# Three plain chunks in the first FFN, and high parts sent out alone in all FFN layers

## The chip, the cores and the metric

The kernel runs on one core of one Trainium2 chip. The metric is the time of one execution on the device in microseconds. Three runs of the kernel before took 1061.67, 1060.71 and 1061.58 us, median 1061.58.

## What is computed

Two decoder layers over 256 tokens of width 1024, in float32: a half-step FFN, an attention mixer (FoX in layer 0, latent attention MLA in layer 1, with a key/value side computed once between), a second half-step FFN and a gated per-layer input, each followed by a layer norm.

```python
def swiglu(x, w_in, w_out):
    h = x @ w_in
    gate, up = h[..., :D_FF], h[..., D_FF:]
    return (jax.nn.silu(gate) * up) @ w_out

for i in range(DEPTH):                       # DEPTH = 2
    if i == N_A:                             # N_A = 1
        k_nope, k_rope, v_shared = shared_kv(x, kv_w_down, kv_norm, kv_w_up, cos, sin)
    x = post_norm(x, 0.5 * swiglu(x, ffn1_w_in[i], ffn1_w_out[i]), ln_g[i, 0], ln_b[i, 0])
    if i < N_A:
        mix = fox_mixer(x, fox_w_in[i], fox_b_f[i], fox_w_o[i])
    else:
        mix = mla_mixer(x, ..., k_nope, k_rope, v_shared, cos, sin)
    x = post_norm(x, mix, ln_g[i, 1], ln_b[i, 1])
    x = post_norm(x, 0.5 * swiglu(x, ffn2_w_in[i], ffn2_w_out[i]), ln_g[i, 2], ln_b[i, 2])
    gate = jax.nn.sigmoid(x @ ple_w_gate[i] + ple_b_gate[i])
    x = post_norm(x, gate * (p[i] @ ple_w_proj[i]), ln_g[i, 3], ln_b[i, 3])
```

post_norm is LN(sqrt(2) * x + delta). D_FF is 2816.

## The kernel before

**Products in three parts.** Each float32 operand of a product is split into a high part (a copy rounded to the matmul's format, made by ScalarE) and a low part (the rest, a subtraction on VectorE). A product is then three matmuls: high by high, high by low, low by high (mm3, L581). So every weight costs ScalarE a "high" and VectorE a "low" before TensorE can use it.

**The stream of weights.** Class Stream (L145) loads weight groups of 1 MB by SyncE's DMA queue, three groups ahead, into raw tiles, and splits them unit by unit (128 x 1024) into ten slots hl0 to hl9 (and homes such as ota, otb, qk, fs when they are lent). A slot comes free once its last product is issued. When the split of a unit is written into the program is decided while the program is generated: after every product, pump (L357) looks at a small clock model. pe_t, act_t and dve_t are the planner's times of TensorE, ScalarE and VectorE; busy (L339) adds to them, for VectorE a fixed 150 ns and 1.05 ns an element. If the raw weight has arrived and the later of act_t and dve_t is at most 1600 ns (SLACK_NS) ahead of pe_t, pump issues the next split (split, L218), both parts together. split(half=True) issues the high alone and leaves the low as self.rest, which later (L208) issues; before the change that is called only by ahead (L192), from close (L801) and from a few places of the mixers' hand-written orders FOX (L49) and ORDER (L71), where "a" is ahead, "l" is later and "f n" fills n units. use (L369) splits at once whatever is still missing when a product needs it. Each engine works through its instructions strictly in the order written.

**An FFN** (ffn, L697) has 11 chunks of 256 hidden columns. HT (L781) computes the gate and the up product of a chunk (each 48 matmuls of 256 columns), close (L801) multiplies silu(gate) by up on VectorE. What follows depends on the chunk:
- plain: the chunk's hidden values are split, and W (L904) multiplies them by w_out at the end of the FFN: 24 matmuls of 512 columns for both token tiles.
- summed: seven products in place of eight (21 matmuls) on sums. add (L814) forms differences of the hidden values (L818, L822, L823) and splits a form of 896 columns; Stream.add (L267) adds up w_out's blocks on VectorE (L273, L279, L281) and then splits four units "ws" (three of 1024 elements, one of 512, in the order 1, 0, 2, 3). sums (L833) then runs the products of a batch of chunks into seven PSUM banks, and product 4 is added to x right away (L858).

In the first FFN (cold) chunk 0 comes first, then the gate and up products of chunks 1 to 4, batch 1 of the sums, chunks 5 to 7, batch 2, chunks 8 to 10 (always plain, STAG = 3), then W. The other FFNs start with both token tiles of chunks 0 and 1 (H, L708) and go on in the same way. Which of the first eight chunks are plain is the tuple early (L705).

Of the kernel before, what the change touches and what calls it, by code (L numbers as in the profile page):

```python
# [28 lines left out]
SLACK_NS = 1600.0  # L29
# [115 lines left out]
class Stream:  # L145


    def __init__(self, nc, raw_pool, pool, loads, seq):
        self.nc, self.raw_pool, self.pool, self.loads = nc, raw_pool, pool, loads
        seen = []  # L150
        self.groups = []
        for key in seq:
            g = group_of(key)
            if g not in seen:
                seen.append(g)
                self.groups.append(g)
        members = {g: [] for g in self.groups}
        self.left = {}
        for key in seq:
            if key not in self.left:  # L160
                self.left[key] = 0
                members[group_of(key)].append(key)
            self.left[key] += 1
        self.order = [k for g in self.groups for k in members[g]]
        self.index = {k: i for i, k in enumerate(self.order)}
        self.last_of = {members[g][-1]: i for i, g in enumerate(self.groups)}
        self.raw, self.hl, self.sums, self.added = {}, {}, {}, {}
        self.slots = [f"hl{i}" for i in range(NSLOT)]
        self.slot_of = {}
        self.kept = set()  # L170
        self.loaded = self.ready = 0
        self.done = 0
        self.pending = None
        self.pe_t = self.act_t = self.dve_t = self.dma_t = 0.0
        self.arrives = {}
        self.between = {}
        self.hold = False
        self.rest = None
        self.at = 0
        self.stop = None  # L180

    def load(self, n=NRAW):
        while self.loaded < len(self.groups) and self.loaded < self.done + n:
# [34 lines left out]
    def split(self, half=False):  # L218
        self.later()
        nc = self.nc  # L220
        key = self.order[self.ready]
        g = group_of(key)
        while self.sums_left(key):
            self.add(g)
        src, parts, n = unit_of(key, self.raw[g], self.sums.get(g))
        slot = self.slots.pop(0)
        self.slot_of[key] = slot
        w = self.place(key, slot)
        hi, lo = w[:parts, 0, :n], w[:parts, 1, :n]
        shape = src.shape  # L230
        if len(shape) == 3:
            hi = hi.rearrange("p (a b) -> p a b", b=shape[2])
            lo = lo.rearrange("p (a b) -> p a b", b=shape[2])
        elif len(shape) == 4:
            hi = hi.rearrange("p (a b c) -> p a b c", b=shape[2], c=shape[3])
            lo = lo.rearrange("p (a b c) -> p a b c", b=shape[2], c=shape[3])
        t = self.arrives[group_of(key)]
        self.act_t, self.dve_t = max(self.act_t, t), max(self.dve_t, t)

        def both():  # L240
            nc.scalar.activation(hi, src, AF.Copy)  # L241
            nc.vector.tensor_tensor(lo, src, hi.bitcast(F32), op=ALU.subtract)  # L242

        if key[0] == "pb":
            nc.gpsimd.memset(w[:, 0, :].bitcast(F32), 0.0)
            lo = w[32:33, 0, :n]
            both()
        elif half:
            nc.scalar.activation(hi, src, AF.Copy)  # L249
            self.busy(act=n)  # L250

            def rest():
                nc.vector.tensor_tensor(lo, src, hi.bitcast(F32), op=ALU.subtract)  # L253
                self.busy(dve=n)
                self.split_done(key, w)

            self.rest = rest
            return
        else:
            both()  # L260
        self.pair(n)
        self.split_done(key, w)
# [76 lines left out]
    def busy(self, act=0, dve=0, pe=0):  # L339
# [1 line left out]
        if act:  # L341
            self.act_t = max(self.act_t, self.pe_t) + 200 + 0.84 * act
        if dve:
            self.dve_t = max(self.dve_t, self.pe_t) + 150 + 1.05 * dve
        if pe:
            self.pe_t += max(109, 0.437 * pe + 4)

# [8 lines left out]

    def pump(self):  # L357

        if self.ready == len(self.order) or not self.slots or self.hold or self.order[self.ready] == self.stop:
            return  # L360
        arrival = self.arrives.get(group_of(self.order[self.ready]), 1e12)
        if arrival <= self.pe_t + 500 and max(self.act_t, self.dve_t) <= self.pe_t + SLACK_NS:
            key = self.order[self.ready]
            if self.sums_left(key):
                self.add(group_of(key))
            else:
                self.split()

    def use(self, key):  # L369
        self.retire()  # L370
        self.load()
        i = self.index[key]
        self.at = max(self.at, i + 1)
        while self.ready <= i:
            assert self.slots, (key, self.slot_of)
            self.split()
            self.pe_t = max(self.pe_t, self.dve_t)
# [106 lines left out]
class Trunk:  # L484
# [212 lines left out]
    def ffn(self, li, which, lni, kv=False, ple=False, at=None, cold=False, after=()):  # L697
# [4 lines left out]
        g, gT, forms = {}, {}, {}  # L702
        homes = HOMES[:3] if kv else HOMES
        S.reclaim(*homes)
        early = (0,) if cold else (0, 1) if kv else (1,)  # L705
        summed = [c for c in range(NCH - STAG) if c not in early]

        def H(c, t, at=None, what=None, sweeps=0):  # L708
# [272 lines left out]
        for c in range(n - STAG, n):  # L981
            W(c, (1,), next_x if c == n - 1 else None)
        self.ln(1, z[1], 1.0, 4 * LN_EPS)

    def room(self, c, summed):
        self.full[c] = f = self.tl([128, 1024], F32, "P", 2)
# [913 lines left out]
```

## Time and profile before

| | us |
|---|---|
| median of three runs | 1061.58 |
| the profiled execution itself | 1060.52 |
| its span in the trace | 1058.7 |

The span runs from the first to the last instruction on the core; the 1.8 us between it and the execution's time lie around it. Times in the trace count from the span's start. The stages as the trace shows them, by the start of their first products:

| stage | from us |
|---|---|
| first FFN, batch 1 of the sums | 60.7 |
| its chunks 5 to 7 | 84.7 |
| batch 2 | 117.8 |
| chunks 8 to 10, then W | 137.5 |
| FoX mixer | 193.3 |
| second FFN of layer 0 | 309.6 |
| second FFN of layer 1 | 841.9 |

PE is TensorE, DVE VectorE, ACT ScalarE. A row of the timeline gives start, length, engine, line, operation, output<-inputs, how many in a row, and in brackets how long the engine was idle before and what released it. Matmuls overlap, so a row's length is more than the time from one start to the next. A window row gives its stretch, its length, an engine's busy time and the TensorE clock granted (1.00 is full).

### The profile page before, as it was taken

The numbers are of one execution on the slowest core, as the hardware profiler recorded it, in microseconds if no ns is written. First come the engines' busy times: TensorE is split into PE (matmuls) and PEld (weight loads), VectorE is DVE, ScalarE is ACT, GpSimd is POOL, SyncE is SP. The second block draws the span as 40 slices with busy tenths as digits, with TensorE's granted clock in tenths as the row PEclk, the third lists the DMA queues.
The fourth block names the chain that finished last, engine by engine and source line by source line (L and its number), as shares of the span: only waits on it lengthen the run. The fifth ranks groups of instructions, "written<-read, shape, count | busy, mean of one in ns | idle before, by whom it ended". The sixth has DMA issues, their size and how long they took to land.

```text
span 1058.7 us, 17610 instructions
## 1 busy us (share of the span) xinstructions
PE 1037.5 (98%) x7091; PEld 949.4 (90%) x7091; DVE 883.9 (83%) x1296; ACT 587.0 (55%) x893; POOL 58.3 (6%) x88
## 2 busy tenths in 40 slices
PE   9999899999999999999999999999999999999996
PEld 8979799898878989998889999988999889899986
DVE  5897887868888889977978799778888889899776
ACT  6555465457846464663564646526776474655631
POOL 0000000113400000000040000000000000000000
PEclk9999999999999999999999999999999999999998
DMA  7846367446447465664575646642444465556522
GB/s 280 316 160 217 141 236 252 155 142 225 161 148 264 174 210 199 212 229 168 207 256 182 210 149 229 232 134 105 136 169 151 168 238 200 187 196 224 205 115 80
DMA packets 37477, 202.74 MB, mean 191 GB/s; under 512 B 3970, under 2 KB 9874, under 8 KB 16532
## 3 DMA queue, kind: packets, MB, share of 16 engines
q1 hardware_dynamic: 37396, 201.63, 53.6%
q8 instruction: 55, 0.90, 0.3%
q14 instruction: 26, 0.21, 0.1%
HBM read 200.55 MB, written 1.06 MB: 190 GB/s over the span
## 4 chain that ended last, share of the span: by engine, by line
PE 70%; ACT 2%; DVE 1%; issue 1%; DVEq 0%; ACTq 0%
PE h L589 37%; PE y L589 23%; PE tr L589 8%; PE tr L593 2%; PE h L593 0%; ACT P L1310 0%; ACT hl L241 0%; ACT qk L602 0%; ACT xT L1603 0%; DVE hl L242 0%; DVE x L681 0%; DVE tr L1685 0%; ACT L570 0%; ACT L757 0%; DVE y L1292 0%
## 5 line engine op out<-in xcount | busy, mean ns | idle before, releaser
L589 PE MATMUL h<-xT,hl 128*128 128x256 f32 x3408 | 394.8, 277 | 0.3 <-DVE hl L302 0.3
L589 PEld LDWEIGHTS h<-xT,hl 128*128 128x128 f32 x3408 | 391.8, 188 | 1.4 <-ACT xT L602 0.6
L242 DVE TENSOR_TENSOR hl<-raw,hl 128x1024 fp32r<-128x1024 f32 (+3 forms) x290 | 338.1, 1197 | 49.0 <-ACT hl L241 47.6
L241 ACT ACTIVATE hl<-raw 128x1024 fp32r<-128x1024 f32 (+3 forms) x290 | 287.7, 1031 | 77.3 <-DVE raw L281 21.9
L589 PE MATMUL y<-hl,g 128*128 128x512 f32 x396 | 92.5, 391 | 0.0
L589 PEld LDWEIGHTS y<-hl,g 128*128 128x128 f32 x396 | 73.7, 188 | 14.8
L589 PE MATMUL y<-hl,otb 128*128 128x512 f32 x264 | 69.3, 395 | 0.0
L589 PE MATMUL h<-hl,xT 128*128 128x512 f32 (+2 forms) x306 | 67.1, 371 | 1.4 <-ACT hl L241 1.4
L589 PEld LDWEIGHTS h<-hl,xT 128*128 128x128 f32 x306 | 53.4, 188 | 11.7 <-ACT hl L241 2.5
L589 PEld LDWEIGHTS y<-hl,otb 128*128 128x128 f32 x264 | 48.1, 188 | 9.5 <-DVE otb L606 0.3
L253 DVE TENSOR_TENSOR hl<-raw,hl 128x1024 fp32r<-128x1024 f32 (+2 forms) x42 | 50.0, 1195 | 2.2 <-ACT hl L249 2.1
L589 PE MATMUL y<-hl,ota 128*128 128x512 f32 x192 | 49.9, 393 | 0.0
L673 POOL TENSOR_TENSOR rs<-ve,mhalf 128x1 f32<-128x1 f32 x16 | 15.1, 943 | 623.5 <-DVE ve L672 623.5
L602 ACT ACTIVATE xT<-tr 128x512 fp32r<-128x512 f32 x28 | 16.1, 596 | 58.2 <-PE tr L593 58.2
L242 DVE TENSOR_TENSOR hl<-ts,hl 128x1024 fp32r<-128x1024 f32 (+1 forms) x52 | 48.0, 962 | 0.2 <-ACT hl L241 0.2
L249 ACT ACTIVATE hl<-raw 128x1024 fp32r<-128x1024 f32 (+2 forms) x42 | 43.1, 1029 | 7.1 <-DVE raw L281 6.1
L589 PE MATMUL tr<-xT,hl 128*128 128x256 f32 x384 | 45.3, 277 | 0.0
L589 PEld LDWEIGHTS tr<-xT,hl 128*128 128x128 f32 x384 | 44.5, 188 | 0.4
L589 PE MATMUL y<-hl,xT 128*128 128x512 f32 (+3 forms) x228 | 43.9, 340 | 0.0
L797 ACT ACTIVATE P<-h 128x512 f32<-128x512 f32 x33 | 19.6, 594 | 41.4 <-PE h L589 41.1
L241 ACT ACTIVATE hl<-ts 128x1024 fp32r<-128x1024 f32 (+1 forms) x52 | 41.9, 839 | 0.0
L589 PEld LDWEIGHTS y<-hl,ota 128*128 128x128 f32 x192 | 34.9, 188 | 6.6
(284 smaller groups left out, 1459.3 us busy)
## 6 DMA issues: line engine op xcount, KB each, us to landing
raw<-in_ffn_in_dram SPq DMA_DIRECT2D x85, 1024.0 KB, 4.9
raw<-in_ffn_out_dram SPq DMA_DIRECT2D x44, 1024.0 KB, 5.0
raw<-in_pg_dram SPq DMA_DIRECT2D x8, 1024.0 KB, 5.6
raw<-in_mo_dram SPq DMA_DIRECT2D x8, 1024.0 KB, 4.7
raw<-in_kq_dram SPq DMA_DIRECT2D x8, 640.0 KB, 4.5
gb<-in_ln_g_dram SPq DMA_DIRECT2D x8, 512.0 KB, 6.7
gb<-in_ln_b_dram SPq DMA_DIRECT2D x8, 512.0 KB, 6.3
raw<-in_fk_dram SPq DMA_DIRECT2D x4, 1024.0 KB, 4.9
```

Of the source, the lines that this page charges most:

```text
L241: nc.scalar.activation(hi, src, AF.Copy)
L242: nc.vector.tensor_tensor(lo, src, hi.bitcast(F32), op=ALU.subtract)
L249: nc.scalar.activation(hi, src, AF.Copy)
L253: nc.vector.tensor_tensor(lo, src, hi.bitcast(F32), op=ALU.subtract)
L589: self.nc.tensor.matmul(out, lhsT, rhs, start=start, stop=stop)
L593: self.nc.tensor.transpose(out, in_, self.ident)
L602: self.nc.scalar.activation(hi, src, AF.Copy)
L673: nc.gpsimd.tensor_tensor(rs, ve, self.mhalf, op=ALU.pow)
L797: nc.scalar.activation(gt, ps, AF.Silu)
```

## The change

It has three parts.

1. In the first FFN three of the first eight chunks are plain (0, 1, 2), not one. Batch 1 of the sums then holds chunks 3 and 4, not 1 to 4, and W takes two more chunks. In the program TensorE has 7082 instructions in place of 7076, VectorE 1282 in place of 1298, ScalarE 823 in place of 827; SyncE and GpSimd keep 251 and 93.
2. In all four FFNs (halves) pump issues a high part alone as soon as ScalarE's model time allows it, whatever VectorE's is; the low part follows at a later pump once VectorE's time allows, or when the weight is used or the next split begins.
3. In the planner's model a VectorE instruction's fixed cost is 80 ns outside the FFNs and stays 150 ns inside. This changes the order only, no instruction's own time.

```diff
+        self.fixed, self.halves = 80, False
...
         elif half:
             nc.scalar.activation(hi, src, AF.Copy)
             self.busy(act=n)
+            done = self.act_t
 
             def rest():
                 nc.vector.tensor_tensor(lo, src, hi.bitcast(F32), op=ALU.subtract)
+                if self.halves:
+                    self.dve_t = max(self.dve_t, done + 100)
                 self.busy(dve=n)
...
-            self.dve_t = max(self.dve_t, self.pe_t) + 150 + 1.05 * dve
+            self.dve_t = max(self.dve_t, self.pe_t) + self.fixed + 1.05 * dve
...
     def pump(self):
 
+        if self.halves and self.rest is not None and not self.hold and self.dve_t <= self.pe_t + SLACK_NS:
+            self.later()
         if self.ready == len(self.order) or not self.slots or self.hold or self.order[self.ready] == self.stop:
             return
         arrival = self.arrives.get(group_of(self.order[self.ready]), 1e12)
-        if arrival <= self.pe_t + 500 and max(self.act_t, self.dve_t) <= self.pe_t + SLACK_NS:
-            key = self.order[self.ready]
-            if self.sums_left(key):
+        if arrival > self.pe_t + 500:
+            return
+        key, late = self.order[self.ready], self.pe_t + SLACK_NS
+        if not self.halves:
+            if max(self.act_t, self.dve_t) <= late:
+                self.split()
+        elif self.sums_left(key):
+            if self.dve_t <= late:
                 self.add(group_of(key))
-            else:
-                self.split()
+        elif self.rest is None and self.act_t <= late:
+            self.split(half=True)
 
     def use(self, key):
...
+        if self.halves and self.ready <= i:
+            self.later()
...
-        early = (0,) if cold else (0, 1) if kv else (1,)
+        S.fixed, S.halves = 150, True
+        early = (0, 1, 2) if cold else (0, 1) if kv else (1,)
...
         self.ln(1, z[1], 1.0, 4 * LN_EPS)
+        S.later()
+        S.fixed, S.halves = 80, False
```

Lines behind the first added one stand lower in the changed kernel (L242 and L253, the low of a split, become L243 and L255; L589 becomes L602, L606 L619, L803 L817, L858 L872).

The order of instructions changes at these places. First, VectorE around the change from chunk 1 to chunk 2 of the first FFN, before and after. L803 (L817) is the closing multiplication of a chunk, which reads its up product from the PSUM bank tr0; raw_161's two units (hl8, hl9) are the weights of chunk 2's gate product, which TensorE runs directly behind tr0.

```order
L242 TENSOR_TENSOR hl7_352<-raw_141,hl7_352 128x1024
L242 TENSOR_TENSOR hl8_357<-raw_161,hl8_357 128x1024
L242 TENSOR_TENSOR hl9_369<-raw_161,hl9_369 128x1024
L803 TENSOR_TENSOR P_325<-P_325,tr0_327 128x512
L818 TENSOR_TENSOR P_325<-P_325 128x256
L822 TENSOR_TENSOR P_325<-P_325 128x128
```

```order
L255 TENSOR_TENSOR hl7_349<-raw_141,hl7_349 128x1024
L817 TENSOR_TENSOR P_325<-P_325,tr0_327 128x512
L255 TENSOR_TENSOR hl8_381<-raw_161,hl8_381 128x1024
L619 TENSOR_TENSOR g4_384<-P_325,g4_384 128x512
L255 TENSOR_TENSOR hl9_395<-raw_161,hl9_395 128x1024
```

The closing of chunk 1 moved ahead of the lows of hl8 and hl9, and the form's additions (L818, L822) are gone from this chunk.

Second, VectorE around the closing of chunk 4, where batch 1 begins on TensorE. L273, L279 and L281 (L277, L283, L285) add up w_out's blocks of one chunk: of chunk 2 before, of chunk 4 after. P_719 and P_703 hold chunk 4's hidden values, whose form's low goes to fs and otb; x0 is updated from product 4.

```order
L273 TENSOR_TENSOR ts_745<-raw_569 128x1024
L279 TENSOR_TENSOR ts_745<-ts_745,raw_569 128x512
L281 TENSOR_TENSOR raw_569<-ts_745,raw_569 128x512
L242 TENSOR_TENSOR hl4_770<-raw_569,hl4_770 128x1024
L803 TENSOR_TENSOR P_719<-P_719,h1_721 128x512
L818 TENSOR_TENSOR P_719<-P_719 128x256
L822 TENSOR_TENSOR P_719<-P_719 128x128
L823 TENSOR_TENSOR P_719<-P_719 128x128
L253 TENSOR_TENSOR hl5_782<-raw_569,hl5_782 128x1024
L606 TENSOR_TENSOR fs_788<-P_719,fs_788 128x896
```

```order
L277 TENSOR_TENSOR ts_766<-raw_593 128x1024
L283 TENSOR_TENSOR ts_766<-ts_766,raw_593 128x512
L285 TENSOR_TENSOR raw_593<-ts_766,raw_593 128x512
L817 TENSOR_TENSOR P_703<-P_703,h1_705 128x512
L832 TENSOR_TENSOR P_703<-P_703 128x256
L836 TENSOR_TENSOR P_703<-P_703 128x128
L837 TENSOR_TENSOR P_703<-P_703 128x128
L255 TENSOR_TENSOR hl4_773<-raw_593,hl4_773 128x1024
L619 TENSOR_TENSOR otb_779<-P_703,otb_779 128x896
L255 TENSOR_TENSOR hl5_793<-raw_593,hl5_793 128x1024
L872 SCALAR_TENSOR_TENSOR x0_69<-x0_69,h0_789 128x512
L255 TENSOR_TENSOR hl6_820<-ts_766,hl6_820 128x1024
```

Chunk 4 is the fourth chunk of the batch before and the second after, so its closing stands three chunks' or one chunk's products ahead of its use.

Third, ScalarE in the FoX mixer, where the probabilities of a pair of heads are transposed (PT, from the PSUM banks tr). The stream takes the weights of keys and queries in turn. raw_2313 before and raw_2137 after hold the same group of query weights, raw_2152 the key weights ahead of it; qk takes generated queries and keys, L1329 (L1345) scales the probabilities P.

```order
L249 ACTIVATE hl7_2527<-raw_2152 128x1024
L602 ACTIVATE qk_2230<-h0_2492 128x256
L249 ACTIVATE hl8_2546<-raw_2152 128x1024
L241 ACTIVATE hl9_2551<-raw_2313 128x1024
L249 ACTIVATE hl3_2555<-raw_2313 128x1024
L602 ACTIVATE PT_2537<-tr1_2538 128x512
L602 ACTIVATE PT_2537<-tr0_2539 128x256
```

```order
L250 ACTIVATE hl2_2515<-raw_2137 128x1024
L615 ACTIVATE qk_2218<-h0_2480 128x256
L250 ACTIVATE hl3_2534<-raw_2137 128x1024
L615 ACTIVATE PT_2525<-tr1_2526 128x512
L615 ACTIVATE PT_2525<-tr0_2527 128x256
L1345 ACTIVATE P_2447<-P_2447,su_2446 128x128
```

Two of the four highs between the earlier products and PT stand further ahead now: the stream comes out of the first FFN one group further on.

## The prediction

> **What bounds the kernel now.** I read the page first (busy shares, then the chain), then the waits of the tensor engine, then windows and the timeline around each wait.
>
> ```profile
> span 1058.7 us, 17610 instructions
> PE 1037.5 (98%) x7091; PEld 949.4 (90%) x7091; DVE 883.9 (83%) x1296; ACT 587.0 (55%) x893; POOL 58.3 (6%) x88
> PE 70%; ACT 2%; DVE 1%; issue 1%; DVEq 0%; ACTq 0%
> 472.04 20.40 PE y L589 x90
> 387.19 31.98 PE h L589 x282
> ```
>
> TensorE (PE) is busy for 98% of the span and holds most of the chain. The two chain pieces give its rate: 90 matmuls of 512 columns in 20.40 us are 0.227 us each, 282 of 256 columns in 31.98 us are 0.113 each. So nothing can be won but PE's own waits, and every added matmul costs its full time unless it fills a wait. The waits of PE come next (what it waited for: us in all, times, longest).
>
> ```profile
> PE y L589 <- DVE hl L242: 4.6, 3, 2.1
> PE tr L589 <- DVE hl L242: 1.5, 2, 1.0
> PE h L589 <- ACT hl L241: 1.4, 2, 0.9
> PE h L589 <- ACT P L1329: 1.0, 1, 1.0
> PE h L589 <- DVE PT L606: 0.9, 2, 0.6
> ```
>
> About 9.4 us in all. The first two rows lie in the first FFN, where its two batches of summed products run. Windows (stretch, length, PE busy, PEclk, DMA share, GB/s) and PE's timeline show them:
>
> ```profile
> 60.68:84.69 24.01, 21.52 (x86) 0.93 0.39 131
> 84.69:117.81 33.12, 32.93 (x289) 1.00 0.55 195
> 117.81:137.46 19.65, 15.56 (x65) 1.00 0.42 155
> ...
> 71.20 1.43 PE L589 MATMUL y<-hl,qk 128*128 128x512 f32 x5 [0.60 <-DVE hl L242]
> 78.39 1.59 PE L589 MATMUL y<-hl,fs 128*128 128x512 f32 x5 [1.89 <-DVE hl L242]
> 131.42 1.45 PE L589 MATMUL y<-hl,qk 128*128 128x512 f32 x5 [2.12 <-DVE hl L242]
> 135.49 0.74 PE L589 MATMUL tr<-hl,qk 128*128 128x512 f32 x2 [1.00 <-DVE hl L242]
> ...
> 79.40:83.00 3.60, 3.60 (x10) 2.78 (x9) 3.07 (x5) 3.60 (x5) 0.00 (x0) 0.53 0.65 203
> ```
>
> Batch 1 is four chunks of 21 matmuls: 84 x 0.227 = 19.0 us of work in 24.0 us, so 5.0 lost. Batch 2 is 63 x 0.227 = 14.3 in 19.65, so 5.4 lost. The last row shows that batch 1 loses in a second way: right after the wait of 1.89 the granted clock is about half (0.53) for 3.6 us, with 10 matmuls where 16 fit, some 1.5 us of the 5.0. The three chunks between the batches (33.1 us, 0.113 x 288 = 32.6) lose next to nothing. VectorE (DVE) is what the batches wait for: it is 22.7 us busy of batch 1's 24.0.
>
> **The first FFN.** A chunk costs 21 matmuls of 512 columns in the summed scheme and 24 in the plain one, so chunks 1 and 2 add 6 x 0.227 = **1.4 us** to PE. They take from VectorE three additions, 1536 elements of low parts and the form's additions each:
>
> ```profile
> L273 DVE TENSOR_TENSOR ts<-raw x27: 1218/1224/1229, 48.5 to 952.1; 128x1024 f32<-128x1024 f32 x27
> L279 DVE TENSOR_TENSOR ts<-ts,raw x27: 691/692/696, 49.7 to 953.4; 128x512 f32<-128x512 f32 x27
> L281 DVE TENSOR_TENSOR raw<-ts,raw x27: 691/692/694, 50.5 to 954.1; 128x512 f32<-128x512 f32 x27
> 24.14 3.50 DVE L242 TENSOR_TENSOR hl<-raw,hl 128x1024 fp32r<-128x1024 f32 x3 [1.80 <-ACT hl L241]
> 28.04 2.20 PE L589 MATMUL h<-xT,hl 128*128 128x256 f32 x18
> 28.24 0.69 DVE L803 TENSOR_TENSOR P<-P,tr 128x512 f32<-128x512 f32 x1 [0.60 <-PE tr L589]
> 28.96 0.42 DVE L818 TENSOR_TENSOR P<-P 128x256 f32<-128x256 f32 x1
> 29.42 0.29 DVE L822 TENSOR_TENSOR P<-P 128x128 f32<-128x128 f32 x1
> 29.75 0.29 DVE L823 TENSOR_TENSOR P<-P 128x128 f32<-128x128 f32 x1
> 53.91 1.08 DVE L606 TENSOR_TENSOR qk<-P,qk 128x896 fp32r<-128x896 f32 x1
> 53.75 1.05 ACT L241 ACTIVATE hl<-raw 128x1024 fp32r<-128x1024 f32 x1
> 52.89 0.96 ACT L602 ACTIVATE qk<-P 128x896 fp32r<-128x896 f32 x1 [4.83 <-DVE P L823]
> ```
>
> A set of additions is 1.22 + 0.69 + 0.69 = 2.6 us, a closing (L803, L818, L822, L823) 1.7, a form's high 0.96 on ScalarE and its low 1.08, a full low about 1.15 in a row (3.50 for three). Per chunk VectorE is spared 2.6 of additions, 1536 elements of lows (1.8) and some 1.4 on the form: 5.8.
>
> *A new wait.* Before, the lows of chunk 2's first two weight slots ran at 24.14, ahead of chunk 1's closing. Now the closing stands ahead of them (first place shown under the change). It needs chunk 1's last product, which ends at 28.04, and PE goes straight to chunk 2, whose third matmul needs that low. So: closing 28.24 + 0.69 = 28.93, low + 1.2 = 30.1, against 28.04 + 2 x 0.113 = 28.27. **PE loses 1.85 us.** Behind the waiting closing stand only that low and later ones, and ScalarE has gone ahead. The second slot's low has 24 matmuls (2.7 us) more and is in time. Bounds: 1.15 (closing and low each 0.35 shorter than their rows) to 2.6 (0.69 more, if the plain chunk's own low slipped ahead).
>
> *Batch 1* now starts at 60.7 + 1.85 = 62.5 with chunks 3 and 4, 42 x 0.227 = 9.5 us. Its three earlier chunk times are 33.1 / 3 = 11.0 each, so chunk 3 closes at 51.5. VectorE from there, in its new order: closing to 53.4, form's high and low to 55.5, additions of chunk 3 to 58.1. Chunk 3's first high stands on ScalarE behind chunk 4's silu, whose product ends at 57.0, and is ready at 58.8; four lows (three full, one 0.69) to 63.0, additions of chunk 4 to 65.6, then chunk 4's closing to 67.3, its form's high to 68.3. PE's seven products of chunk 3 last to 67.3: **1.0 wait.** The form's low follows a weight's low and ends at 69.7, where PE wants it at 68.8: 0.8. The low for product 5 stands behind the update of x (L858, as long as L803's 0.69) that needs product 4: 1.0. In all 2.8 us lost in place of 5.0, a gain of **2.2**.
>
> *Batch 2* has the same seven rows per chunk as before; its highs go out earlier and its additions keep their place. The same count gives waits of 0.7, 2.1 and 0.5, so 3.3 lost in place of 5.4: **2.1**. For both batches together the ends are 0 lost (the additions done ahead of the batch) and 10.4 (as before); I take 6.1, since the additions of each next chunk still stand behind the lows.
>
> First FFN: 2.2 + 2.1 - 1.85 - 1.4 = **1.0 us** gained.
>
> **The mixer and the second FFNs.** At 242 us PE waits for the transposed probabilities (PT) of the FoX heads:
>
> ```profile
> 239.40 1.05 ACT L249 ACTIVATE hl<-raw 128x1024 fp32r<-128x1024 f32 x1
> 240.35 1.05 ACT L241 ACTIVATE hl<-raw 128x1024 fp32r<-128x1024 f32 x1
> 241.29 1.05 ACT L249 ACTIVATE hl<-raw 128x1024 fp32r<-128x1024 f32 x1
> 242.25 0.85 ACT L602 ACTIVATE PT<-tr 128x512 fp32r<-128x512 f32 x2
> 243.50 1.59 PE L589 MATMUL h<-PT,g 128*128 128x512 f32 x6 [1.03 <-ACT P L1329]
> ```
>
> Three highs stand ahead of PT from 239.40 on; two of them are gone from there (third place under the change), having run earlier. PT is then up to 1.9 us sooner, which covers the wait of 1.03 and some 0.2 that the next low costs: **1.2**. Bounds: 0 if ScalarE fills the place with another high, 1.5.
>
> Both second FFNs start with a wait for a weight's high (two rows of the chain, then the timeline; the last two are layer 1's):
>
> ```profile
> 315.37 1.28 ACT L757 ACT_TABLE_LOAD   x1 [5.63 <-PE h L589]
> 316.67 0.39 ACT L757 ACTIVATE P<-h 128x256 f32<-128x256 f32 x1
> 318.05 1.21 PE L589 MATMUL h<-hl,xT 128*128 128x512 f32 x4 [0.92 <-ACT hl L241]
> ...
> 847.92 0.96 ACT hl L241
> 848.92 0.74 PE L589 MATMUL h<-hl,xT 128*128 128x512 f32 x2 [0.51 <-ACT hl L241]
> ```
>
> ScalarE sat idle for 5.63 us before the table load: the planner held both parts of the split back until VectorE, too, had time. Issued alone, one more high of 1.05 runs in that gap, ahead of x's transposes. Gain 0.92 and 0.51, each with about 0.1 lost at the next low: **1.0 and 0.6**. What may be late next is the low of x's transposed copy, pushed by at most one low (1.15). Bounds: 0 and 1.6.
>
> The Trainium skill, "ScalarE: Activation LUTs" (What ACT_TABLE_LOAD costs), gives a switch of function set about 2.66 us, 1.28 of load and 1.38 of drain. The row has the 1.28, and silu starts 0.02 us behind it, so no run here shows the second part; by the page the gap that the high now fills would still be long enough.
>
> At the border of the first FFN and FoX two more lows stand ahead of a low of x (0.1 lost) while x's second half is sooner (0.2 gained): **0.1**. The rest of the mixers, key/value and per-layer parts keep their order but for a shift or two, off PE's waits, and cost nothing while VectorE has slack there; without it, one low of 1.15 each.
>
> **Sum:** 1.0 + 1.2 + 1.0 + 0.6 + 0.1 = 3.9 us. The profiled run took 1060.5 (span 1058.7 and 1.8 around it), so 1056.6 for a run like it. The median of the runs shown is 1.06 higher, 1061.58; from there **1057.7**. About 0.2% (2.1 us) is what a measurement of this kernel can tell from no change.
>
> **Rivals.** *1: the clock.* After an idle of 1.89 us PE's clock was half for a stretch, after the 2.12 in batch 2 it was not. The forecast has two waits of that size, at 28 and in batch 2. If each brings a stretch, 2 x 1.5 = 3.0 is lost beside the forecast's own: 1060.7; with one, 1059.2. For it: one of two such waits did. Against: only one of two. The Trainium skill, "TensorE: Matmul & The Clock Gate" (HAM oscillation), asks for idle gaps above about 3.4 us for this; by that rule batch 1 could not have dropped and both waits would be free of it. The row of 0.53 says otherwise, so the rival keeps its chance.
>
> *2: full recovery.* With less on VectorE, the additions are finished ahead of the batches and 6.1 us of waits more go: 1051.6, half of it 1054.6. For: 2 x 5.8 = 11.6 us of VectorE work leave. Against: within a batch the order, not the load, makes the waits.
>
> *3: only the first FFN gains*: highs issued alone do not reach the starts in time, or another takes their place, so the 2.9 us outside stay: 1060.6. For: ScalarE is free early only if the raw weight has landed. Against: it sat idle 5.6 us there.
>
> *4: slower.* What makes the wait at 28 is general: a high goes out, its low is put off behind a closing that needs PE's newest product. If this happens at the first chunk change of the other three FFNs as well, each at 1.85 or up to 2.6, and twice in one, the loss is 4 x 1.85 = 7.4: 1057.7 + 7.4 = 1065.1. It turns the sign from the third place on (5.6 > 3.9). For: the same code runs in all four. Against: there ScalarE and VectorE are not behind from a cold start, and in their instruction order the low that PE needs next stands ahead of the closing.
>
> **Chances.** Forecast 0.46 (1055.5 to 1059.4), clock 0.16, full recovery 0.14, first FFN only 0.12, slower 0.12. A quarter of the clock case (one stretch) still counts as faster: 0.46 + 0.14 + 0.04 = 0.64 faster, 0.12 + 0.12 = 0.24 same, 0.12 slower. The range runs from halfway into the recovery case, 1053.5, to 1062.5, which leaves out most of the slower case and a few chances in a hundred below.
>
> **What would show it.** Of the changed kernel: a PE wait on VectorE of about 1.9 at 28 us and PEclk 1.00 behind it; first batch about 12.3 us long, second about 17.6; no wait on L1329's row near 240, none on a weight's high at the starts of the second FFNs. It is wrong if PE's waits elsewhere in the later FFNs come up, or if a stretch of half clock appears.

## The result and the profile after

The changed kernel took 1065.39 us, median of six runs (1063.79 to 1067.29), against 1061.12 for the kernel before, also six runs: 1.0042 times as long, 95% interval 1.0029 to 1.0055. It is slower by 4.3 us where 3.9 us faster was forecast, outside the range and on the other side. The profiled execution took 1065.16, its span is 1063.4.

The page's first lines and the longest waits of TensorE after (what PE waited for: us in all, times, longest):

```profile
span 1063.4 us, 17599 instructions
PE 1042.5 (98%) x7097; PEld 951.8 (90%) x7097; DVE 872.2 (82%) x1280; ACT 584.4 (55%) x889; POOL 57.4 (5%) x88
PE h L602 <- DVE hl L255: 2.9, 3, 1.7
PE y L602 <- DVE hl L243: 1.8, 1, 1.8
PE tr L602 <- DVE hl L255: 1.3, 2, 1.0
PE y L578 <- POOL mhalf L563: 1.2, 1, 1.2
PE h L606 <- DVE x L872: 1.0, 1, 1.0
PE y L602 <- ACT otb L615: 0.8, 1, 0.8
```

Two things are to be read here. The waits have hardly shrunk: all rows of this view add up to 11.9 us, before to 12.3. And PE's busy time grew by 5.0 us, for which six more matmuls of 0.227 account for only 1.4. So 3.6 us at least are matmuls that take longer; it is more, since some 1.6 us of the busy time before came from the half-clock stretch in batch 1, which the profile after does not have. The critical chain shows where: products (y, six matmuls each) on the form kept in otb, in the batch at 367 us, whose products the change leaves as they are. Before, then after:

```profile
371.76 1.36 PE y L589 x6
376.52 1.36 PE y L589 x6
...
371.32 1.39 PE y L602 x6
376.20 1.39 PE y L602 x6
```

A summed chunk of 21 matmuls takes 4.76 us before and 4.88 after, 232 ns a matmul in place of 227. In the first FFN it is the 256-column matmuls; the view that groups them by shape gives their durations (shortest, median, longest, in ns) between 31 and 59 us, before and after:

```profile
L589 PE MATMUL h<-xT,hl x250: 276/276/276, 30.8 to 59.0; 128*128 128x256 f32 x125
L602 PE MATMUL h<-xT,hl x240: 281/281/281, 30.8 to 59.0; 128*128 128x256 f32 x120
```

Every one takes 5 ns more; from one start to the next it is 118 where it was 113. The usual step from one matmul's start to the next is taken here as the median for its shape in the kernel before (113 ns at 256 columns, 227 at 512, 109 at 128). Adding up over the whole trace what each step lags behind that, the lags of up to 60 ns grow by 5.7 us, and the longer ones, which are waits, the half clock and fixed steps between unlike matmuls, shrink by 2.4. With 1.4 us of added products that is 5.7 - 2.4 + 1.4 = 4.7, the difference of the two spans. Of the 2.4, 1.6 is the half-clock stretch, so the waits themselves shrank by only 0.8 us.

The waits that the prediction spoke of, in PE's timeline after:

```profile
28.17 0.39 PE L602 MATMUL h<-xT,hl 128*128 128x256 f32 x2
30.25 2.03 PE L602 MATMUL h<-xT,hl 128*128 128x256 f32 x15 [1.69 <-DVE hl L255]
...
64.03 1.54 PE L602 MATMUL y<-hl,ota 128*128 128x512 f32 x6
69.78 0.74 PE L602 MATMUL y<-hl,otb 128*128 128x512 f32 x2 [0.81 <-ACT otb L615]
70.94 1.19 PE L602 MATMUL y<-hl,otb 128*128 128x512 f32 x4 [0.42 <-DVE otb L619]
74.75 0.73 PE L602 MATMUL tr<-hl,otb 128*128 128x512 f32 x2 [0.99 <-DVE hl L255]
76.72 0.86 PE L602 MATMUL h<-xT,hl 128*128 128x256 f32 x6
...
109.83 1.54 PE L602 MATMUL y<-hl,ota 128*128 128x512 f32 x6
...
123.43 1.42 PE L602 MATMUL y<-hl,qk 128*128 128x512 f32 x5 [1.83 <-DVE hl L243]
128.18 0.87 PE L602 MATMUL h<-xT,hl 128*128 128x256 f32 x6
...
244.37 1.21 PE L602 MATMUL h<-PT,g 128*128 128x512 f32 x6
315.88 2.91 PE L602 MATMUL h<-hl,xT 128*128 128x512 f32 x12
...
856.32 0.97 PE L602 MATMUL h<-hl,xT 128*128 128x512 f32 x3 [0.76 <-DVE hl L255]
922.25 0.66 PE L606 MATMUL h<-ident,g 128*128 128x128 f32 x4 [1.04 <-DVE x L872]
```

The wait at 28, those of the batches, and the two that go (244 and 316 have none) are there much as written. The wait at the start of layer 1's second FFN is gone, but the one at 856, for a low, is new and stands only some 5 us further on (11.8 us behind the FFN's first product, where the old one stood 6.6 behind it). The one at 922 is new as well: four lows in a row stand ahead of the update of x that frees a PSUM bank, where three stood before.

### The profile page after: what moved, and what is told of

Its sections match the earlier page's. It is cut to its first block, busy times and chain, and to the rows that moved or that the text cites. A ratio compares the mean times of both kernels' runs of the same rounds, so it can differ in the third digit from the quotient of the medians.

```text
span 1063.4 us, 17599 instructions
## 1 busy us (share of the span) xinstructions
PE 1042.5 (98%) x7097; PEld 951.8 (90%) x7097; DVE 872.2 (82%) x1280; ACT 584.4 (55%) x889; POOL 57.4 (5%) x88
## 4 chain that ended last, share of the span: by engine, by line
PE 65%; DVE 6%; ACT 1%; issue 1%; POOL 0%; DVEq 0%; ACTq 0%; POOLq 0%
PE h L602 34%; PE y L602 22%; PE tr L602 7%; DVE hl L255 2%; PE tr L606 2%; DVE ts L277 0%; PE h L606 0%; DVE x L694 0%; DVE hl L243 0%; DVE ts L283 0%; DVE raw L285 0%; ACT hl L250 0%; DVE P L817 0%; DVE st L676 0%; DVE tr L1701 0%
## 5 line engine op out<-in xcount | busy, mean ns | idle before, releaser
L602 PE MATMUL h<-xT,hl 128*128 128x256 f32 x3384 | 394.3, 278 | 2.1 <-DVE hl L255 1.7
L602 PEld LDWEIGHTS h<-xT,hl 128*128 128x128 f32 x3384 | 390.5, 188 | 4.1 <-DVE hl L255 1.9
L255 DVE TENSOR_TENSOR hl<-raw,hl 128x1024 fp32r<-128x1024 f32 (+1 forms) x285 | 335.5, 1207 | 43.0 <-ACT hl L250 41.3
L250 ACT ACTIVATE hl<-raw 128x1024 fp32r<-128x1024 f32 (+1 forms) x285 | 285.9, 1041 | 81.4 <-PE y L602 27.2
L602 PE MATMUL y<-hl,g 128*128 128x512 f32 x432 | 100.3, 390 | 0.0
L602 PEld LDWEIGHTS y<-hl,g 128*128 128x128 f32 x432 | 80.6, 188 | 16.3
L602 PE MATMUL y<-hl,otb 128*128 128x512 f32 x264 | 70.9, 399 | 1.9 <-ACT otb L615 0.8
L602 PE MATMUL h<-hl,xT 128*128 128x512 f32 (+2 forms) x300 | 65.5, 371 | 0.8 <-DVE hl L255 0.8
L602 PEld LDWEIGHTS h<-hl,xT 128*128 128x128 f32 x300 | 52.4, 188 | 10.5 <-DVE hl L255 1.2
L602 PEld LDWEIGHTS y<-hl,otb 128*128 128x128 f32 x264 | 48.0, 188 | 13.2 <-ACT otb L615 1.2
L243 DVE TENSOR_TENSOR hl<-raw,hl 128x1024 fp32r<-128x1024 f32 (+4 forms) x46 | 50.5, 1116 | 8.9 <-ACT hl L242 8.4
L602 PE MATMUL y<-hl,ota 128*128 128x512 f32 x192 | 49.9, 394 | 0.0
L602 PE MATMUL y<-hl,xT 128*128 128x512 f32 (+3 forms) x258 | 47.8, 333 | 0.0
L242 ACT ACTIVATE hl<-raw 128x1024 fp32r<-128x1024 f32 (+4 forms) x46 | 43.6, 970 | 4.9 <-DMA raw<-in_ffn_in_dram 3.5
L255 DVE TENSOR_TENSOR hl<-ts,hl 128x1024 fp32r<-128x1024 f32 (+1 forms) x50 | 45.7, 953 | 0.5 <-ACT hl L250 0.2
L602 PE MATMUL tr<-xT,hl 128*128 128x256 f32 x384 | 45.3, 277 | 0.3 <-DVE hl L255 0.3
L602 PEld LDWEIGHTS tr<-xT,hl 128*128 128x128 f32 x384 | 44.5, 188 | 0.7 <-DVE hl L255 0.5
L602 PEld LDWEIGHTS y<-hl,xT 128*128 128x128 f32 x258 | 39.7, 188 | 4.5 <-ACT xT L615 0.4
L602 PEld LDWEIGHTS y<-hl,ota 128*128 128x128 f32 x192 | 34.9, 188 | 6.6
```

Of the source, the lines that this page charges most:

```text
L602: self.nc.tensor.matmul(out, lhsT, rhs, start=start, stop=stop)
```

## The experiments

The two kernels' order of instructions does not say why matmuls on otb are slow, so the tiles' places were compared. Where an SBUF tile lies follows from the order in which the program first asks for each tile name. Chunk 4 asks for gb just before its products; before, otb and qk had been asked for by the forms of chunks 2 and 3, now no form of theirs exists and gb comes first. Places in bytes, and what is left over 256:

```
tile        before        after
hl0..hl9    ... 224       the same
xT          11936  160    11936  160
ota         155104 224    155104 224
otb         163552 224    178016  96
qk          178144 224    186464  96
gb          186784 160    163616  32
```

**Where the tiles lie.** *aligned*: the changed kernel, with three names asked for ahead of gb, so that all tiles lie as before.

```diff
         if first:
+            self.tl([128, 2, 896], F32R, "otb", 1)
+            self.tl([128, 1536], F32, "ts", 1)
+            self.tl([128, 2, 896], F32R, "qk", 1)
             self.tl([128, 16], F32, "gap0", 1)
```

> The changed kernel, with the tiles otb, ts and qk allocated ahead of gb, so that every SBUF tile lies at the address it had before (otb at 163552, not 178016; qk at 178144, not 186464; gb at 186784, not 163616). The order of instructions is the changed kernel's. Theory A (place of the tiles: matmuls that read otb, qk or gb are some 5 ns slower each where these tiles lie 128 bytes off the other slots in steps of 256): products on otb and qk go back from 230.7 to 226.7 ns, 4.2 us less than the changed kernel, about 1061. Theory B (the new order of VectorE's and ScalarE's work slows the matmuls beside it): no change, about 1065.3. Under both the waits at 28, 70, 115 to 122, 855 and 921 us stay.

Measured 1062.88, 1.0015 times the kernel before (1.0005 to 1.0025): 2.5 us less than the changed kernel. *before_moved* is the other way round, the kernel before with gap0, gb, gap1 and ts asked for ahead of otb, at the changed kernel's addresses.

```diff
             tag, o = self.home(homes)
+            if cold and c == 1:
+                self.tl([128, 16], F32, "gap0", 1)
+                self.tl([128, 2, D], F32, "gb", 1)
+                self.tl([128, 16], F32, "gap1", 1)
+                self.tl([128, 1536], F32, "ts", 1)
```

> The kernel before, with its tiles otb, ts, qk and gb allocated at the addresses of the changed kernel; the order of instructions stays. Theory A: products on otb and qk at 230.7 ns in place of 226.9, some 4 us slower than the kernel before, about 1065. Theory B: the same as before, 1061.1.

Measured 1063.31, 1.0018 (1.0009 to 1.0028). The same chain pieces, of aligned and then of before_moved:

```profile
371.74 1.36 PE y L602 x6
376.50 1.36 PE y L602 x6
...
370.39 1.39 PE y L589 x6
375.27 1.39 PE y L589 x6
```

4.76 and 4.88 us a chunk: the products follow the addresses, whatever the order. Theory B is out for these products. The times move by 2.5 and 2.1 us, not by the 4 expected. In the trace of before_moved the short lags, counted as above, are 3.6 us more than in the kernel before, close to the 4. One reason why the time moves less is in the profiles. The half clock that the kernel before shows behind a wait of 2 us is missing in before_moved at the same place, though the wait is there, and aligned has one at another place, behind a wait of 1.89 that the changed kernel has too (1.83), without it. The windows right behind these waits, of before_moved and of aligned (PEclk is the third from the end):

```profile
78.00:82.00 4.00, 3.74 (x16) 3.09 (x17) 3.93 (x6) 4.00 (x6) 0.00 (x0) 1.00 0.34 94
122.00:126.00 4.00, 3.13 (x10) 2.46 (x11) 3.93 (x5) 4.00 (x5) 0.00 (x0) 0.75 0.21 43
```

Such a stretch costs about 1.6 us, so one execution's difference can be off by that. How much of the gap between 4 and 2 it makes in the medians stays open. *moved_256* moves the kernel before by 256 bytes.

```diff
+            if cold and c == 2:
+                self.tl([128, 64], F32, "shift", 1)
             tag, o = self.home(homes)
```

> The kernel before with otb, ts, qk, gb and all tiles behind them 256 bytes further on; the order stays. If what counts is the place within 256 bytes: products on otb and qk at 226.7 to 227 ns, the same time as before. If any move away from the old addresses costs: 230.7 ns as in 'before_moved'.

One run, 1063.12; the kernel before took 1058.54 to 1063.44 in 17 runs beside it, so this one time says nothing for or against. The profile does: the products on otb are fast (chain pieces 4.76 us apart again), so a move of 256 bytes does not slow them, as expected. Its span is still 1.9 us longer than that of the kernel before, and the reason does not lie in those products. The matmuls of chunks 5 to 7, in moved_256 and in the kernel before,

```profile
L589 PE MATMUL h<-xT,hl x264: 280/281/364, 85.9 to 117.0; 128*128 128x256 f32 x132
L589 PE MATMUL h<-xT,hl x275: 276/276/367, 85.8 to 116.9; 128*128 128x256 f32 x138
```

are of the slow kind in one execution and of the fast kind in the other, with one order and one place within 256 bytes. It is some 1.4 us for one such stretch. The half clock, too, came twice here, behind both waits of about 2 us, where the kernel before had it once; this is the second:

```profile
132.00:136.00 4.00, 3.60 (x11) 2.92 (x12) 2.46 (x4) 3.74 (x5) 0.00 (x0) 0.72 0.36 84
```

**The wait at 28 and what followed it.** *aligned_low_first* writes one low ahead of the closing.

```diff
             S.ahead()
+            if cold and c == 1:
+                S.later()
             nc.vector.tensor_tensor(gt, gt, up, op=ALU.mult)
```

> As the kernel 'aligned', and at the end of chunk 1 of the first FFN the low of chunk 2's first weight is written ahead of the closing multiplication. Theory C (a wait in a run of 256-column matmuls also leaves PE at 117.8 ns a matmul until wider products come): 1.85 us of wait and 1.4 us of slower matmuls from 30.6 to 64.5 us go, 3.2 us less than 'aligned', matmuls of 113.3 ns there. Rival D (the slower matmuls from 30.6 to 64.5 come from the new order of lows there): only the wait goes, 1.9 us less, matmuls stay at 117.8.

Measured 1060.60, 0.9994 (0.9985 to 1.0002): 2.3 us less than aligned. The wait of 1.7 us is replaced by one of 0.6 at the next weight:

```profile
27.82 3.22 PE L602 MATMUL h<-xT,hl 128*128 128x256 f32 x26
31.64 0.61 PE L602 MATMUL h<-xT,hl 128*128 128x256 f32 x3 [0.59 <-DVE hl L255]
```

For the slow stretch neither theory holds. In aligned, which has the full wait at 28, the matmuls behind it took 276; here they took 276 as well, but those of chunks 5 to 7 took 281. So that wait is not what makes the stretch. All profiles here together show what goes with it: between 10 and 62 us the rate changes, to the slow side or back, only at a short stop of PE, a step of 0.22 us or more in place of 0.113. aligned turned from slow to fast at its wait at 30.7, the changed kernel from fast to slow at the same wait, at 30.3, moved_256 from slow to fast at one step of 0.22 at 25.6. Other such stops changed nothing.

**High parts alone.** *one_plain* is the changed kernel with one plain chunk.

```diff
-        early = (0, 1, 2) if cold else (0, 1) if kv else (1,)
+        early = (0,) if cold else (0, 1) if kv else (1,)
```

> The changed kernel with one plain chunk among the first eight, as before: high parts alone and the mixers' own VectorE cost stay. The tiles then lie, in steps of 256 bytes, as before. If my terms outside the first FFN hold (FoX 1.5, start of layer 0's second FFN 1.2, start of FoX 0.3, less the new waits at 855 and 921 us of 0.3 and 1.2 and 0.3 at 413): 1.2 us faster than before there, about 1060, and whatever the first FFN makes of high parts alone. If the slower matmuls come from high parts alone (theory B), about 1064.

Measured 1065.63, 1.0039 (1.0025 to 1.0053), far from both 1060 and, in its cause, from theory B: its matmuls are fast. It waits. At 31 us PE waits 2.8 us for a low, and the FoX wait is back, which the plain chunks had taken away:

```profile
30.98 1.30 PE L602 MATMUL h<-xT,hl 128*128 128x256 f32 x5 [2.79 <-DVE hl L255]
246.43 1.35 PE L602 MATMUL h<-PT,g 128*128 128x512 f32 x4 [0.93 <-ACT P L1345]
```

*plain_only* has the three plain chunks and nothing else of the change (the kernel before with early = (0, 1, 2) and the three names asked for early).

> The kernel before with three plain chunks (0, 1, 2) among the first eight of the first FFN and nothing else of the change; otb, ts and qk are allocated ahead of gb, so that all tiles lie as before in steps of 256 bytes. Theory E (the plain chunks pay, since they take 11.6 us of VectorE work out of the stretch where PE waits for it, and high parts sent alone are what costs): no wait near 28 us, 1.4 us more products, batch waits down from 10.4 to about 6 us: 2 to 3 us faster than before, 1058 to 1059. Rival F (VectorE's order, not its load, makes the waits, so plain chunks only add products): 1 to 1.5 us slower, about 1062.5.

Measured **1050.67, 0.9901 (0.9884 to 0.9918): 10 us faster than before**, four times what theory E expected. *whole_cold* is aligned with highs and lows issued together in the first FFN alone.

```diff
-        S.fixed, S.halves = 150, True
+        S.fixed, S.halves = 150, not cold
```

> The kernel 'aligned' with highs and lows issued together, as before, in the first FFN alone; the other three FFNs keep high parts alone. Theory E: the 1.85 us wait at 28 goes; the FoX wait near 243 and the start wait of layer 0's second FFN stay away; the waits near 851 (0.9) and 917 (1.4) us stay: 1.9 us less than 'aligned', about 1061, and about 1 us less than before plus what 'plain_only' gains. Rival F: as 'aligned' or above.

Measured 1052.76, 0.9917 (0.9901 to 0.9933): 10 us less than aligned, again far more than the 1.9 expected. So, with three plain chunks, high parts alone in the first FFN cost 10 us and eat what the plain chunks gain. The gain of plain_only fits what the prediction counted as lost: 10.4 us in the two batches and 1.2 in FoX, less 1.4 for the added products, make 10.2. Windows of plain_only around batch 1 and batch 2 (columns: stretch, length, busy time of PE, PEld, DVE, ACT, POOL, PEclk, DMA share, GB/s) show PE busy throughout but for 0.2 us:

```profile
60.00:72.50 12.50, 12.50 (x70) 10.86 (x69) 12.40 (x16) 9.22 (x10) 0.00 (x0) 1.00 0.40 121
105.00:120.00 15.00, 14.84 (x76) 12.31 (x75) 14.72 (x19) 9.91 (x12) 0.00 (x0) 1.00 0.45 145
```

And from 28 to 62 us, ahead of batch 1, VectorE's window and what it waits for, in the changed kernel and then in plain_only:

```profile
28.00:62.00 34.00, 32.31 (x274) 32.12 (x274) 23.67 (x26) 17.21 (x21) 0.00 (x0) 1.00 0.70 268
DVE hl L255 <- ACT hl L250: 5.9, 4, 3.4
DVE P L817 <- PE tr L602: 2.9, 1, 2.9
DVE P L817 <- PE h L602: 2.2, 2, 1.7
...
28.00:62.00 34.00, 34.00 (x295) 33.72 (x295) 27.87 (x31) 18.75 (x22) 0.00 (x0) 1.00 0.80 293
DVE hl L242 <- ACT hl L241: 4.1, 4, 2.4
DVE P L806 <- PE tr L589: 0.6, 1, 0.6
DVE P L806 <- PE h L589: 0.3, 1, 0.3
```

By 62 us VectorE has 4.2 us less done from 28 on. Batch 1 itself begins at 64.0 us in the changed kernel and at 60.4 in plain_only; counted from 8 us to there, VectorE has done 37.5 and 40.3 us, so 2.8 less although it had 3.7 us more time. It stood at closings that wait for PE (2.9 + 2.2 against 0.9 us) and at highs. Work that needs nothing from PE, above all the additions of chunk 3, stands behind them; the first of the additions begins at 56.8 us in the changed kernel and at 48.2 in plain_only:

```profile
L277 DVE TENSOR_TENSOR ts<-raw x25: 1217/1224/1226, 56.8 to 956.0; 128x1024 f32<-128x1024 f32 x25
L273 DVE TENSOR_TENSOR ts<-raw x25: 1218/1224/1227, 48.2 to 941.7; 128x1024 f32<-128x1024 f32 x25
```

*plain_sums_late* tests that: plain_only, with the additions of chunk 3, and what follows them in the stream, kept behind its closing.

```diff
+        if cold:
+            S.stop = ("ws", li, which, 3, 1)
...
-        if self.ready == len(self.order) or not self.slots or self.rest is not None:
+        if self.ready == len(self.order) or not self.slots or self.rest is not None or self.order[self.ready] == self.stop:
             return
...
                 add(c)
+                if cold and c == 3:
+                    S.stop = None
                 return
```

> The kernel 'plain_only', in which the additions of chunk 3's sums may not be written ahead of chunk 3's closing; in the changed kernel they stood behind it and began at 56.8 us, in 'plain_only' ahead of it at 48.2. Theory G (the waits of batch 1 come from VectorE's additions and lows starting late, not from their number): 1.5 to 3 us of PE waits come back in batch 1, about 1053; batch 2 stays without. Rival (VectorE catches up, because its load is lower): no wait in batch 1 above 0.3 us, 1050.7.

Measured 1055.01, 0.9941 (0.9925 to 0.9957). Two waits come back in batch 1, the first two that the changed kernel has there; batch 2 stays without:

```profile
68.57 0.73 PE L589 MATMUL y<-hl,otb 128*128 128x512 f32 x2 [1.51 <-ACT otb L602]
69.72 1.20 PE L589 MATMUL y<-hl,otb 128*128 128x512 f32 x4 [0.42 <-DVE otb L606]
```

Theory G holds for batch 1, whose load on VectorE is the same as in plain_only. The time rose by 4.3 us, and the waits explain some 2 of it; the profiled execution also has two stretches of slow matmuls (7 to 62 and 74 to 109 us), 2.9 us of short lags, that plain_only's has not.

**The other FFNs and the mixers' cost.** *low_first_last_whole*: aligned_low_first, with whole splits in the second FFN of layer 1.

```diff
-        S.fixed, S.halves = 150, True
+        S.fixed, S.halves = 150, (li, which) != (1, "ffn2")
```

> The kernel 'aligned_low_first' with highs and lows issued together in the second FFN of layer 1. If the waits near 851 (0.94 us) and 917 (1.45 us) come from lows put off there: both go, the start wait of before (0.67) comes back, 1.7 us less than 'aligned_low_first', about 1059. If they come from elsewhere: no change, 1060.6.

Measured 1060.66, 0.9998 (0.9987 to 1.0008), no gain. Both waits go, but the start's own comes back larger than in the kernel before, 1.6 us:

```profile
850.38 0.97 PE L602 MATMUL h<-hl,xT 128*128 128x512 f32 x3 [1.63 <-ACT hl L242]
```

*plain_half_l0*: plain_only with high parts alone in the second FFN of layer 0 only.

> The kernel 'plain_only' with high parts alone in one FFN, the second of layer 0, where the start wait of 1.09 us went in every run with them. Theory E (highs alone cost where the planner then lets VectorE stand behind them, and gain where ScalarE stands idle at the start of an FFN): that wait goes and nothing else comes, 1.1 us less than 'plain_only', 1049.6. If high parts alone cost in any FFN: above 1051.

Measured 1057.32, 0.9960 (0.9947 to 0.9973), 6.6 us above plain_only; a slow stretch from 10 to 62 us, which plain_only's profile has not, is 2 us of it in the profiled execution. The start wait did not go, and new ones came: 0.40 us at 314 and 0.83 at 379 in that FFN, the second of them before an update of x as at 922 in the changed kernel, and two behind it, in the per-layer input's transposes and at the start of the next FFN:

```profile
509.60 0.63 PE L606 MATMUL tr<-ident,x 128*128 128x128 f32 x4 [0.76 <-DVE x L697]
523.29 0.97 PE L602 MATMUL h<-hl,xT 128*128 128x512 f32 x3 [2.41 <-DVE hl L243]
```

*plain_mixer_cost* is plain_only with 80 ns as VectorE's fixed cost outside the FFNs, and *plain_fox_cost* with 80 ns in the FoX mixer alone.

> The kernel 'plain_only' with the third part of the change alone beside it: the planner's fixed cost of a VectorE instruction is 80 ns outside the FFNs. It moves a few lows and highs of the mixers by one place. Expected: the same as 'plain_only' within 0.5 us (1050.7), since the FoX wait near 231 (1.19 before) is gone without it already; if the mixers' order was what cost in the changed kernel, 1.5 us or more above.

> The kernel 'plain_only' with the planner's fixed VectorE cost of 80 ns from the end of the first FFN to the start of layer 0's second FFN (the FoX mixer) and 150 ns everywhere else. In 'plain_mixer_cost' the start wait of layer 0's second FFN (1.09 us) was gone and that of layer 1's was 1.8 in place of 0.7. Theory H (the first comes from the FoX mixer's cost, the second from the MLA mixer's): start of layer 0 without a wait, start of layer 1 at 0.7: 1.0 us less than 'plain_only', 1049.7. Rival (the order downstream shifts anyway): a wait comes back at some other place, 1050.7 or more.

Measured 1051.82, 0.9905 (0.9892 to 0.9918), and **1049.84, 0.9893 (0.9875 to 0.9910)**. The start wait of layer 0's second FFN is there in plain_only and gone in plain_fox_cost, though both split whole in that FFN:

```profile
307.56 1.21 PE L589 MATMUL h<-hl,xT 128*128 128x512 f32 x4 [0.92 <-ACT hl L241]
...
305.70 2.92 PE L602 MATMUL h<-hl,xT 128*128 128x512 f32 x12
```

In plain_mixer_cost it is gone too, but layer 1's start wait is 1.6 us, where plain_only and plain_fox_cost have 0.5. Theory H holds in the profile: the planner's lower cost in the FoX mixer takes the first wait away, and the same cost behind it, up to the end of the MLA mixer, makes the second longer. plain_fox_cost is the fastest version here, 11 us or 1.1% ahead of the kernel before; its lead over plain_only is within what the runs tell apart.

## Why the prediction was wrong, point by point

- *The rate of matmuls.* This step failed, and it cost the most. The sum took 0.227 and 0.113 us from the kernel before for every matmul after, and slower matmuls stand in it at nothing; of the rest of the program it said that it costs nothing as long as its order stays. The order stayed, the places of otb, qk and gb did not. Steps slower than usual cost 5.7 us in the profiled execution: some 3.6 go with the places (before_moved has these without the change) and 1.2 are the slow stretch from 30.6 to 64 us, a kind that other executions show elsewhere or not at all. In that sum it turned the sign, for without it the span would be 1.0 us shorter than before. No row of the kernel before and no row of the order shows an address; it has to be looked up.
- *The waits as a whole.* This step failed too: with the places put back, aligned is still 1.7 us slower than the kernel before, and PE's waits add up to 12.1 us there against 12.3. The lags of over 60 ns, place by place (after less before, the half clock included), beside the forecast:

| place | forecast | measured |
|---|---|---|
| up to 33 us, with the wait at 28 | +1.85 | +2.2 |
| batch 1 | -2.2 | -1.8 |
| batch 2 | -2.1 | -1.4 |
| border and FoX | -1.3 | -2.1 |
| second FFN of layer 0 | -1.0 | -0.9 |
| second FFN of layer 1 and behind it | -0.6 | +1.6 |
| sum | -5.35 | -2.4 |

  Elsewhere nothing was forecast and they differ by less than 0.1. The one place with the wrong sign is layer 1's second FFN. In batch 1 nearly all of the gain is the half-clock stretch (1.6 us), which this execution did not have.
- *The wait at 28.* Right: 1.85 forecast, 1.85 measured from start to start (30.25 - 28.28 less 0.11). A smaller one of 0.3 at 25 us, also for a low, was not forecast.
- *The batches.* Near: 12.3 us forecast for batch 1 and 12.7 measured, 17.6 and 18.3 for batch 2, with three waits in each, as counted. But the reading of it failed: these waits were taken for the rest of the old ones, and full recovery was given 0.14 because "within a batch the order, not the load, makes the waits". That is half true: with splits issued whole, the plain chunks take the waits away, and it was the change's own second part that made an order in which they did not. The order counts even then: plain_sums_late, with the same load on VectorE, has two of the waits back. Without the second part the plain chunks reach 1050.67. That the rival said 1051.6 is partly luck: its sum held 1.85 us lost at 28 and 1.7 gained outside the first FFN beside FoX, neither of which plain_only has, and they nearly cancel.
- *FoX.* Right in place and size (the 1.2 and more are gone); plain_only has it without the two other parts, and one_plain, which has them without the plain chunks, keeps the wait. So it belongs to the plain chunks.
- *Start of layer 0's second FFN.* The gain of 1.0 came, the reason was wrong: not a high sent alone but the FoX mixer's cost (plain_half_l0 keeps the wait, plain_fox_cost has none).
- *Start of layer 1's second FFN.* Wrong: 0.6 gain forecast, for the wait of 0.51 went, but one of 0.76 came some 5 us further on, for a low. And what the fourth rival feared, a wait for VectorE in a later FFN, came there once, at 922, for 1.0 us; it was looked for at chunk changes only, not at the update of x. With splits issued whole in that FFN both go (low_first_last_whole), but the start's own wait is then 1.6 us, so nothing is won.
- *The clock.* The profiled execution shows no clock below 1.00 from 30.6 us to the end of batch 2, in spite of waits of 1.7 and 1.8 us. With one order of instructions, a half clock followed one of two waits of about 2 us in the kernel before, none of two in before_moved, both in moved_256. The length of the wait does not decide it either: 2.41 us at 523 in plain_half_l0 left the clock at 1.00, and 2.79 at 31 in one_plain did not (0.57 from 31 to 35 us). So it differs between executions, as the rival took it. The Trainium skill, "TensorE: Matmul & The Clock Gate" (HAM oscillation), asks for idle gaps above about 3.4 us; by that rule none of these stretches could have come, and here the runs decide.

The parts, from the runs: plain chunks -10.1 us, high parts alone in the first FFN +10.1, the other FFNs and mixers +2.1 (whole_cold against plain_only), addresses +2.5. The sum is +4.6, the result +4.3; each of these medians carries an interval of about 1 us or more to either side, and whole_cold's profile has some 1.6 us of slow matmuls that plain_only's has not. This is also only one order of taking the parts: with high parts alone in all FFNs the plain chunks are worth 2.7 us (one_plain against aligned), not 10.1, and high parts alone in one later FFN cost 6.6 us in plain_half_l0 (its slow stretch included), where whole_cold has them in three for 2.1. What a part is worth depends on the others.

What stays open: why one stop of PE turns a run of 256-column matmuls from 113 to 118 ns apart, or back, and another does not; why the medians of aligned and before_moved move by 2 to 2.5 us where the steps in the trace say 3.6; and what in the planner's clock makes high parts alone let VectorE fall behind (its waits and the late additions are shown, the decision that causes them is only read from the code: the next unit is not looked at until the last low is written).

## What to carry to other kernels

Before trusting a rate from the old trace, compare the addresses of all tiles that TensorE reads: a tile that is first asked for elsewhere shifts every later one. Test a change's parts apart before judging the whole; here one part was worth 1% and another took it back. An early start for one engine can be worth nothing if what it feeds stands behind an instruction that waits for the engine to be helped.

## What the runs showed of the hardware

- Where a tile lies can change the rate of its products. The weight slots begin at 224 within 256 bytes. 512-column products on otb and qk took 232 ns from start to start with these tiles at 96 and 227 with them at 224 (4.88 and 4.76 us for 21), and those on gb 233 with gb at 32 and 229 with it at 160. A move by 256 bytes left them at 227 and 229 (one run). It is not just a distance of 128 bytes between the two operands, since gb lies 64 from the slots, counted around the 256, at either place; and 256-column products of xT (160) on otb (96) stayed at 113. Which places are slow in general is not shown.
- A run of 256-column matmuls has two rates, 113 and 118 ns apart, and stayed in one for some 400 matmuls (11.5 to 60 us in whole_cold, about 2 us). Between 10 and 62 us it changed, in either direction, only at a stop of PE of 0.1 us or more, and several such stops changed nothing.
- The clock's half stretches differ between executions, too: 0.72 and 0.75 in windows of 4 us behind waits of about 2 us, in some executions and not in others of the same order.
